# q's projection of six head pairs in the 512-column form, and the scaling of all probabilities on one engine

## The chip, the cores and the metric

The kernel runs on one core of a Trainium2 chip. The core has a matrix engine (TensorE, PE in the rows; its weight loads are listed apart as PEld), three engines for elementwise work (VectorE or DVE, ScalarE or ACT, GpSimd or POOL), and DMA queues that one more engine (SyncE, SP) starts. Each engine works through its own list of instructions in order and waits on semaphores for the others. The metric is the device time of one execution in microseconds, as the median of several runs.

## The reference

One layer of a decoder: RMS norm, 16-head causal attention over 256 positions with model width 1024, a residual, RMS norm, a gated feed-forward block of width 2816 with a causal three-tap convolution, a residual, and a last norm. With a sequence of 256 and blocks of 256 there is one block only, so the block choice of the attention drops out and what is left of it is

```
hn  = rmsnorm(x, norm_mix)
q   = hn @ Wq * 64**-0.5 ;  k = hn @ Wk ;  v = hn @ Wv      # 16 heads of 64
p   = softmax(causal(q @ k.T))                              # per head, 256 x 256
x   = x + (p @ v) @ w_o
x   = x + conv_ffn(rmsnorm(x, norm_ffn))
out = rmsnorm(x, norm_final)
```

All inputs and outputs are float32.

## The kernel before

Every large product is made from two parts of each operand: a high part (a copy rounded to the format that TensorE takes, written by ACT) and a low part (the operand minus its high part, written by DVE). Three matmuls then add up high x high, high x low and low x high in PSUM (`mm3`, lines 231 to 235). The transposed input lies in one tile `XT`, for each of its 8 slices of 128 rows the high part (256 columns) and right beside it the low part (256 columns).

There are two ways to project a weight slice. The narrow one (`proj`, line 244) issues three matmuls of 256 columns per slice. The wide one, used by the feed-forward block for its columns 3 to 20 (lines 579 to 581), issues one matmul of 512 columns, high weights times high and low input side by side, and one of 256 columns, low weights times high input. It leaves the sum in two halves of a PSUM bank, which are added on DVE afterwards (lines 635 and 636).

The attention works on pairs of heads, 0 to 7. The projections of pairs 0 and 1 are done while the first data arrive. Pairs 2 to 7 are done in ticks (`qk_tick`, line 483); between the ticks of pairs 5 and 6 stands one value tick, which projects the second half of v. A tick projects q (`A`) and k (`B`) of its pair, and in between does the scores and softmax of the pair two back and the transposes and p x v of the pair three back. What follows the tick of pair 7 is written out in a closing list, `LAST`.

The order is a list, `SCHED`, of named steps with a lag: lag 1 means that the step belongs to the tick before. Each step goes to the end of the lists of the engines that it uses, so the list fixes the order on every engine:

```
("OL", 1), ("KH", 1), ("QL", 1), ("H0", 0), ("KL", 1), ("L0", 0), ("A", 0), ("TR", 0), ("H1", 0),
("SC", 0), ("TH", 0), ("MX", 0), ("E0", 0), ("E1", 0), ("TL", 0), ("RC", 0), ("QH", 0), ("L1", 0),
("N0", 0), ("B", 0), ("KF", 0), ("N1", 0), ("H2", 0), ("PV", 0), ("OH", 0), ("L2", 0)
```

On ACT run `H` (high part of weights, line 180), `KH` and `QH` (high parts of k and q, lines 288 and 276), `E0`, `E1` (the exponentials, 321), `TH` (high part of the transposed probabilities, 346) and `OH` (high part of p x v, 362). On DVE run `L` (low part of weights, 183), `KF`, `KL`, `QL` (scaling of k, low parts of k and q; 284, 292, 280), `MX` (mask and maximum, 311), `RC` (reciprocal of the sums, 325), `TL` (349) and `OL` (367). The probabilities of query rows 0 to 127 and 128 to 255 are scaled by the reciprocals in `N0` (ACT, 128 columns, line 331) and `N1` (DVE, 256 columns, line 333), two instructions each. On TensorE the scores of a pair (`SC`) take as weights first the high part of k, and with their second matmul its low part, which `KL` writes; p x v takes with its second matmul the low part of the transposed probabilities, which `TL` writes.

Of the kernel before, what the change touches and what calls it, by code (L numbers as in the profile page):

```python
# [10 lines left out]
AF = mybir.ActivationFunctionType  # L11
ALU = mybir.AluOpType
AX = mybir.AxisListType

P = 128
S = 256
D = 1024
KT = D // P
# [32 lines left out]
def hybrid_layer(ctx: ExitStack, tc: tile.TileContext, a):  # L51
    nc = tc.nc
    pe, dve, act, pool = nc.tensor, nc.vector, nc.scalar, nc.gpsimd
# [7 lines left out]
    def f32(t):  # L61
        return t.bitcast(F32)

    def psA():
        return ps.tile([P, 512], F32, name="psA", tag="A", bufs=4)

    def psS(i):
        return ps.tile([P, 512], F32, name=f"psS{i}", tag=f"S{i}")
# [36 lines left out]
    XT = cst.tile([P, KT, 2, S], F32R, name="XT")  # L105
    XTh, XTl = XT[:, :, 0, :], XT[:, :, 1, :]
# [103 lines left out]
    QK = [Unit(a["wqk"][j - 2] if j > 1 else None, 2048, 2) for j in range(NP)]  # L210
    VW = [Unit(a["wv"][i], 2048, 2) for i in range(4)]
    WO = [Unit(a["wo"][j], 1024, 1) for j in range(NP)]
    UP = [Unit(a["wup"][c], 2048, 2) for c in range(NC)]
# [17 lines left out]
    def mm3(out, l, r, first, last):  # L231
        (lh, ll), (rh, rl) = l, r
        pe.matmul(out, lh, rh, start=first, stop=False)  # L233
        pe.matmul(out, lh, rl, start=False, stop=False)  # L234
        pe.matmul(out, ll, rh, start=False, stop=last)  # L235
# [8 lines left out]
    def proj(out, unit, k, off):  # L244
        h, l = unit.v(unit.hi, KT), unit.v(unit.lo, KT)
        mm3(out[:, :S], (h[:, k, off:off + P], l[:, k, off:off + P]), (XTh[:, k, :], XTl[:, k, :]),
            k == 0, k == KT - 1)
# [9 lines left out]
    def bcast_R(c, alloc):  # L257

        rp = alloc()
        for t in range(2):  # L260
            pe.transpose(rp[:, t * P:(t + 1) * P], st[:, c + t:c + t + 1].to_broadcast([P, P]), ident)
        act.activation(R, rp[:, :S], AF.Copy)
# [6 lines left out]
    qps, kps, SP, PR, PT, OP = {}, {}, {}, {}, {}, {}  # L269
    KF, QH, QL = {}, {}, {}  # L270
# [7 lines left out]
    def q_lo(j):  # L278
        QL[j] = wk.tile([P, S], F32R, name="QL", tag="ml", bufs=3)
        dve.tensor_sub(QL[j], qps[j][:, :S], f32(QH[j]))  # L280

    def k_evac(j):
        KF[j] = wk.tile([P, S], F32, name="KF", tag="QT")
        dve.tensor_mul(KF[j], kps[j][:, :S], R)

    def k_hi(j):
        for h in range(2):
            act.activation(KMh[j % 2][rows[h], h, :], KF[j][rows[h], :], AF.Copy)

    def k_lo(j):  # L290
        for h in range(2):
            dve.tensor_sub(KMl[j % 2][rows[h], h, :], KF[j][rows[h], :], f32(KMh[j % 2][rows[h], h, :]))
# [34 lines left out]
    def softmax_norm(j, t):  # L327
        for h in range(2):
            r = sm[j][:, 4 + 2 * t + h:5 + 2 * t + h]
            if t == 0:  # L330
                act.activation(PR[j][:, h, 0:P], PR[j][:, h, 0:P], AF.Copy, scale=r)
            else:
                dve.tensor_scalar(PR[j][:, h, P:P + S], PR[j][:, h, P:P + S], r, None, op0=ALU.mult)

    def transp(j):
        PT[j] = psT()
# [32 lines left out]
    def v_mm(half, part, vp, ts=(0, 1), kks=range(4)):  # L369
        u = VW[2 * half + part]  # L370
        h, l = u.v(u.hi, 4), u.v(u.lo, 4)
        for t in ts:
            for kk in kks:
                k = 4 * part + kk
                tk = slice(t * P, (t + 1) * P)
                mm3(vp[t], (XTh[:, k, tk], XTl[:, k, tk]), (h[:, kk, :], l[:, kk, :]), k == 0, k == KT - 1)
# [5 lines left out]
    def v_lo(half, vp, t):  # L382
        c = slice(half * 512, (half + 1) * 512)
        dve.scalar_tensor_tensor(Vl[:, t, c], vp[t], st[:, 2 + t:3 + t], f32(Vh[:, t, c]),
                                 op0=ALU.mult, op1=ALU.subtract)

    def qproj(j):
        qps[j] = psA()
        for k in range(KT):
            proj(qps[j], QK[j], k, 0)  # L390

    def kproj(j):
        kps[j] = psA()
# [7 lines left out]
    for k in range(KT):  # L401
        c = slice(S * k, S * k + S)
# [25 lines left out]
    def halves(u, key):  # L428
        return {f"{n}{key}{i}": (lambda f=f, i=i: f(i)) for n, f in (("H", u.split_hi), ("L", u.split_lo)) for i in range(u.n)}

    def scales():
# [3 lines left out]
    start = {"V0": lambda: v_mm(0, 0, vp), "V1": lambda: v_mm(0, 1, vp, (0,), (0, 1)), "V2": lambda: v_mm(0, 1, vp, (0,), (2, 3)),  # L435
             "V3": lambda: v_mm(0, 1, vp, (1,)), "KH0": lambda: k_hi(0), "KL0": lambda: k_lo(0),
             "RS": scales, "BC": lambda: bcast_R(2, lambda: psS(0)), **halves(VW[1], "V"), **halves(QK[2], "Q")}
    for i in range(2):
        start |= {f"QH{i}": lambda i=i: q_hi(i), f"QL{i}": lambda i=i: q_lo(i), f"KF{i}": lambda i=i: k_evac(i),
                  f"SS{i}": lambda i=i: ssq(x_sb[:, i, :], i, x1[:, i, :]),  # L440
                  f"VH{i}": lambda i=i: v_hi(0, vp, i), f"VL{i}": lambda i=i: v_lo(0, vp, i)}
# [19 lines left out]
    def steps(a_mm, b_mm, j, s_j, t_j, nxt):  # L461
        nxt = [(u, i) for u in nxt for i in range(u.n)]
        d = {"A": a_mm, "B": b_mm, "SC": lambda: scores(s_j), "MX": lambda: softmax_dve(s_j),
             "E0": lambda: softmax_exp(s_j, 0), "E1": lambda: softmax_exp(s_j, 1),
             "RC": lambda: softmax_recip(s_j), "N0": lambda: softmax_norm(s_j, 0), "N1": lambda: softmax_norm(s_j, 1),
             "KH": lambda: k_hi(s_j + 1), "KL": lambda: k_lo(s_j + 1)}
        for n, (u, i) in enumerate(nxt):
            d[f"H{n}"], d[f"L{n}"] = (lambda u=u, i=i: u.split_hi(i)), (lambda u=u, i=i: u.split_lo(i))
        if j is not None:
            d |= {"QH": lambda: q_hi(j), "QL": lambda: q_lo(j), "KF": lambda: k_evac(j)}  # L470
        if t_j is not None:
            d |= {"TR": lambda: transp(t_j), "TH": lambda: pt_hi(t_j), "TL": lambda: pt_lo(t_j), "PV": lambda: pv(t_j),
                  "OH": lambda: o_hi(t_j), "OL": lambda: o_lo(t_j)}
        return d
# [8 lines left out]
    def qk_tick(j, *args):  # L483
        tick(lambda: qproj(j), lambda: kproj(j), j, *args)
# [51 lines left out]
    for i in range(5):  # L536
        last[f"W{i}"] = lambda i=i: wo_all(i)
    last |= {"SC": lambda: scores(7), "MX": lambda: softmax_dve(7), "E0": lambda: softmax_exp(7, 0),
             "E1": lambda: softmax_exp(7, 1), "RC": lambda: softmax_recip(7), "N0": lambda: softmax_norm(7, 0),
             "N1": lambda: softmax_norm(7, 1), "Hc0": up2, "Lc0": lambda: UP[2].split_lo(0)}  # L540
    for i in (6, 7):
        last |= {f"TR{i}": lambda i=i: transp(i), f"TH{i}": lambda i=i: pt_hi(i), f"TL{i}": lambda i=i: pt_lo(i),
# [5 lines left out]
    gps = {}  # L548
# [19 lines left out]
    def wide(c):  # L568
        return 3 <= c < NC - 1


    def up(c, g, ks):
        if (c, g) not in gps:
            gps[c, g] = psA()
        for k in ks:
            if not wide(c):
                proj(gps[c, g], UP[c], k, g * P)
                continue
            h, l = (UP[c].v(t, KT)[:, k, g * P:(g + 1) * P] for t in (UP[c].hi, UP[c].lo))
            pe.matmul(gps[c, g], h, XT[:, k], start=k == 0, stop=False)  # L580
            pe.matmul(gps[c, g][:, :S], l, XTh[:, k, :], start=False, stop=k == KT - 1)  # L581

    for t in range(2):
        wo_mm(5, t, 0)
# [17 lines left out]
    UP[2].split_lo(1)  # L602
    xtr(1, 0)
    up(0, 0, range(4))
    xtr(1, 1)
    up(0, 1, range(4))
    up(1, 0, range(4))
    xsplit(1, (0, 1))
    xsplit(1, (2, 3))
# [235 lines left out]
```

## Time and profile before

| what | us |
|---|---|
| three runs | 314.21, 313.17, 313.20 |
| their median | 313.20 |
| the profiled execution, its own time | 313.81 |
| its span, first to last instruction | 312.1 |
| from the transposes of pair 6's tick to those of pair 7's | 8.49 |

The profile lists, for one execution, the busy time of each engine, the groups of instructions by line with their mean time and the idle time before them, and the chain of work that ended last. In the timeline each row is a start, a duration, the engine and line, output and input tiles, and in brackets how long the engine had sat idle and who released it. A matmul's duration overlaps with the next one; the spacing of starts is what it takes of TensorE. The granted TensorE clock was 0.997 of full speed over the span.

### The profile page before, as it was taken

To read this page: it belongs to the slowest core of one execution; us is meant where nothing else is said; L and a number is where in the kernel's file an instruction comes from. 1 tells how busy PE (TensorE), PEld (TensorE's weight loads), DVE (VectorE), ACT (ScalarE), POOL (GpSimd) and SP (SyncE) were. 2 spreads that over 40 slices of the span, in tenths; PEclk is the share of its full clock that TensorE was granted. 3 is DMA by queue.
4 is the path that set the end of the run, shared out by engine and by line. 5 is a ranking of instruction groups with operands and counts; after the bars stand their busy time and mean duration, and the time that the engine had idled before them with its cause. 6 is when DMAs were issued, how large, how long until landed. Compare 5 with 4: busy or idle time off the path is not lost.

```text
span 312.1 us, 4927 instructions
## 1 busy us (share of the span) xinstructions
PE 303.9 (97%) x1789; PEld 267.1 (86%) x1789; DVE 260.6 (84%) x515; ACT 213.4 (68%) x406; POOL 8.1 (3%) x26
## 2 busy tenths in 40 slices
PE   8899999999999999999999999999999999999991
PEld 5888999988998889998888888888888888888981
DVE  3776888977999977389998999998888888886885
ACT  5786878877989827477767777676666666664423
POOL 5000000000000000000000000000000000000021
PEclk9999999999999999999999999999999999999998
DMA  6999453873041594428764666555555511220003
GB/s 202 369 412 376 159 172 105 318 260 137 1 143 61 186 413 169 177 72 345 246 213 169 212 218 210 204 203 190 165 191 197 204 67 68 69 67 0 3 0 134
DMA packets 13944, 55.47 MB, mean 178 GB/s; under 512 B 1376, under 2 KB 4704, under 8 KB 10208
## 3 DMA queue, kind: packets, MB, share of 16 engines
q1 hardware_dynamic: 13344, 54.30, 48.0%
q10 hardware_dynamic: 576, 0.85, 0.8%
q8 instruction: 14, 0.23, 0.3%
q14 instruction: 10, 0.08, 0.1%
HBM read 54.10 MB, written 1.05 MB: 177 GB/s over the span
## 4 chain that ended last, share of the span: by engine, by line
PE 94%; DMA 2%; DVE 1%; SPq 1%; ACT 0%; issue 0%; DVEq 0%
PE psA L580 21%; PE psA L581 11%; PE psA L235 11%; PE psA L233 11%; PE psA L234 11%; PE psT L235 4%; PE psT L234 4%; PE psT L233 4%; PE psS L234 4%; PE psS L235 4%; PE psS L233 4%; DMA head<-in_first 2%; PE psT L339 2%; PE psA L415 1%; PE psA L419 1%; PE psA L417 1%
## 5 line engine op out<-in xcount | busy, mean ns | idle before, releaser
L580 PE MATMUL psA<-XT,whi 128*128 128x512 f32 x144 | 50.8, 393 | 0.0
L233 PE MATMUL psA<-XT,whi 128*128 128x256 f32 x144 | 40.8, 283 | 0.0
L235 PE MATMUL psA<-XT,wlo 128*128 128x256 f32 x144 | 40.6, 282 | 0.0
L234 PE MATMUL psA<-XT,whi 128*128 128x256 f32 x144 | 40.6, 282 | 0.0
L581 PE MATMUL psA<-XT,wlo 128*128 128x256 f32 x144 | 40.6, 282 | 0.0
L183 DVE TENSOR_TENSOR wlo<-head,whi 128x1024 fp32r<-128x1024 f32 x32 | 38.7, 1218 | 2.1 <-ACT whi L180 2.1
L648 DVE SCALAR_TENSOR_TENSOR y<-pad,head,y 128x256 f32<-128x256 f32 x86 | 36.1, 479 | 1.3 <-ACT y L643 1.3
L183 DVE TENSOR_TENSOR dlo<-rawd,dhi 128x1024 fp32r<-128x1024 f32 x29 | 35.3, 1218 | 0.1
L643 ACT ACTIVATE y<-pad,head 128x256 f32<-128x256 f32 x43 | 25.4, 598 | 13.6 <-DVE pad L637 10.2
L180 ACT ACTIVATE whi<-head 128x1024 fp32r<-128x1024 f32 x32 | 33.1, 1048 | 0.1
L580 PEld LDWEIGHTS psA<-XT,whi 128*128 128x128 f32 x144 | 27.0, 188 | 6.2
L180 ACT ACTIVATE dhi<-rawd 128x1024 fp32r<-128x1024 f32 x29 | 30.2, 1048 | 2.6 <-PE psA L235 2.1
L580 PE MATMUL psA<-XT,OTh 128*128 128x512 f32 x80 | 28.2, 393 | 0.0
L233 PEld LDWEIGHTS psA<-XT,whi 128*128 128x128 f32 x144 | 27.1, 189 | 0.4
L234 PEld LDWEIGHTS psA<-XT,whi 128*128 128x128 f32 x144 | 27.1, 188 | 0.4
L581 PEld LDWEIGHTS psA<-XT,wlo 128*128 128x128 f32 x144 | 27.1, 188 | 0.4
L235 PEld LDWEIGHTS psA<-XT,wlo 128*128 128x128 f32 x144 | 27.1, 188 | 0.0
L636 DVE TENSOR_TENSOR pad<-psA,pad 128x256 f32<-128x256 f32 x36 | 15.2, 423 | 13.8 <-ACT pad L635 13.8
L580 PE MATMUL psA<-XT,Vh 128*128 128x512 f32 x64 | 22.6, 393 | 0.0
L581 PE MATMUL psA<-XT,OTl 128*128 128x256 f32 x80 | 22.5, 282 | 0.0
L635 ACT ACTIVATE pad<-psA 128x256 f32<-128x256 f32 x36 | 12.7, 372 | 13.5 <-PE psA L581 13.5
L714 ACT ACTIVATE sact<-y 128x256 f32<-128x256 f32 x21 | 8.8, 419 | 16.9 <-DVE y L648 16.9
(201 smaller groups left out, 754.1 us busy)
## 6 DMA issues: line engine op xcount, KB each, us to landing
head<-in_wup SPq DMA_DIRECT2D x12, 1024.0 KB, 4.8
rawd<-in_wdn SPq DMA_DIRECT2D x22, 512.0 KB, 3.4
raw<-in_wup SPq DMA_DIRECT2D x10, 1024.0 KB, 4.8
raw<-in_wqk SPq DMA_DIRECT2D x4, 1024.0 KB, 7.5
rawd<-in_wo SPq DMA_DIRECT2D x8, 512.0 KB, 3.6
raw<-in_wv SPq DMA_DIRECT2D x4, 512.0 KB, 8.8
head<-in_wv SPq DMA_DIRECT2D x2, 1024.0 KB, 5.0
head<-in_first SPq DMA_DIRECT2D x5, 384.0 KB, 7.5
```

Of the source, the lines that this page charges most:

```text
L180: act.activation(self.hi[:, c], self.raw[:, c], AF.Copy)
L183: dve.tensor_sub(self.lo[:, c], self.raw[:, c], f32(self.hi[:, c]))
L233: pe.matmul(out, lh, rh, start=first, stop=False)
L234: pe.matmul(out, lh, rl, start=False, stop=False)
L235: pe.matmul(out, ll, rh, start=False, stop=last)
L580: pe.matmul(gps[c, g], h, XT[:, k], start=k == 0, stop=False)
L581: pe.matmul(gps[c, g][:, :S], l, XTh[:, k, :], start=False, stop=k == KT - 1)
L635: act.activation(u, v[:, S:], AF.Copy)
L636: dve.tensor_add(u, v[:, :S], u)
L643: act.activation(y[c, g], pads[c % 2][g][:, 2:S + 2], AF.Identity, scale=cw[:, 2, g * NC + c:g * NC + c + 1], bias=cb[:, g * NC + c:g * NC ...
L648: dve.scalar_tensor_tensor(y[c, g], pads[c % 2][g][:, j:j + S], cw[:, j, col:col + 1], y[c, g], op0=ALU.mult, op1=ALU.add)
L714: act.activation(sact, y[c, 0], AF.Silu)
```

## The change

For pairs 2 to 7 q's projection is issued in the wide form (a new `proj_wide`, now used by the feed-forward block too). q's high part is taken from the first half of the PSUM bank as before; to q's low part the second half is added by one more DVE instruction. `N1` goes from DVE to ACT, at the same place of `SCHED` and `LAST`; so all scaling of probabilities is on ACT. k's projection, pairs 0 and 1, and everything behind the attention compute as before. Lines after line 280 shift by a few.

```diff
     def q_lo(j):
         QL[j] = wk.tile([P, S], F32R, name="QL", tag="ml", bufs=3)
         dve.tensor_sub(QL[j], qps[j][:, :S], f32(QH[j]))
+        if j > 1:
+            dve.tensor_add(QL[j], qps[j][:, S:], f32(QL[j]))
...
     def softmax_norm(j, t):
         for h in range(2):
             r = sm[j][:, 4 + 2 * t + h:5 + 2 * t + h]
-            if t == 0:
-                act.activation(PR[j][:, h, 0:P], PR[j][:, h, 0:P], AF.Copy, scale=r)
-            else:
-                dve.tensor_scalar(PR[j][:, h, P:P + S], PR[j][:, h, P:P + S], r, None, op0=ALU.mult)
+            c = slice(0, P) if t == 0 else slice(P, P + S)
+            act.activation(PR[j][:, h, c], PR[j][:, h, c], AF.Copy, scale=r)
...
+    def proj_wide(out, unit, k, off):
+        h, l = (unit.v(t, KT)[:, k, off:off + P] for t in (unit.hi, unit.lo))
+        pe.matmul(out, h, XT[:, k], start=k == 0, stop=False)
+        pe.matmul(out[:, :S], l, XTh[:, k, :], start=False, stop=k == KT - 1)
+
     def qproj(j):
         qps[j] = psA()
         for k in range(KT):
-            proj(qps[j], QK[j], k, 0)
+            proj_wide(qps[j], QK[j], k, 0)
```

On ACT, in the tick of pair 6, before (`QH` is q's high part of pair 6, `dhi` the high part of a weight of the output projection, `OTh` that of p x v, `KMh_88` that of k):

```order
L276 ACTIVATE QH<-psA 128x256
L331 ACTIVATE PR<-PR,sm 128x128 x2
L180 ACTIVATE dhi<-rawd 128x1024
L362 ACTIVATE OTh<-psA 64x256 x2
L288 ACTIVATE KMh_88<-KF 64x256 x2
L180 ACTIVATE dhi<-rawd 128x1024 x2
L346 ACTIVATE pth<-psT 128x768
```

and now:

```order
L276 ACTIVATE QH<-psA 128x256
L333 ACTIVATE PR<-PR,sm 128x128 x2
L333 ACTIVATE PR<-PR,sm 128x256 x2
L180 ACTIVATE dhi<-rawd 128x1024
L362 ACTIVATE OTh<-psA 64x256 x2
L290 ACTIVATE KMh_88<-KF 64x256 x2
L180 ACTIVATE dhi<-rawd 128x1024 x2
```

The two scalings of 256 columns stand ahead of the weight's high part, and all that follows is behind them.

On DVE, same tick, before (`dlo` is the low part of that weight, `KMl_90` the low part of k that the next scores take):

```order
L325 RECIPROCAL sm<-sm 128x4
L183 TENSOR_TENSOR wlo<-raw_128,whi 128x1024
L284 TENSOR_TENSOR KF<-psA,R 128x256
L333 TENSOR_SCALAR PR<-PR,sm 128x256 x2
L183 TENSOR_TENSOR dlo<-rawd,dhi 128x1024
L367 TENSOR_TENSOR OTl<-psA,OTh 64x256 x2
L280 TENSOR_TENSOR QL<-psA,QH 128x256
L292 TENSOR_TENSOR KMl_90<-KF,KMh_88 64x256 x2
```

and now:

```order
L327 RECIPROCAL sm<-sm 128x4
L183 TENSOR_TENSOR wlo<-raw_128,whi 128x1024
L286 TENSOR_TENSOR KF<-psA,R 128x256
L183 TENSOR_TENSOR dlo<-rawd,dhi 128x1024
L367 TENSOR_TENSOR OTl<-psA,OTh 64x256 x2
L280 TENSOR_TENSOR QL<-psA,QH 128x256
L282 TENSOR_TENSOR QL<-psA,QL 128x256
L294 TENSOR_TENSOR KMl_90<-KF,KMh_88 64x256 x2
```

The scalings are gone, and the addition to q's low part stands between that low part and the low part of k.

On ACT, in the closing list, after the last exponentials (pair 7), before (`pth` is the high part of pair 6's transposed probabilities):

```order
L321 ACTIVATE PR,sm<-PR,mx 128x128 x2
L321 ACTIVATE PR,sm<-PR,mx 128x256 x2
L346 ACTIVATE pth<-psT 128x768
L180 ACTIVATE whi<-head 128x1024
L331 ACTIVATE PR<-PR,sm 128x128 x2
```

and now:

```order
L323 ACTIVATE PR,sm<-PR,mx 128x128 x2
L323 ACTIVATE PR,sm<-PR,mx 128x256 x2
L333 ACTIVATE PR<-PR,sm 128x256 x2
L346 ACTIVATE pth<-psT 128x768
L180 ACTIVATE whi<-head 128x1024
```

The scaling of pair 7 stands ahead of the high part of pair 6, and it has to wait for the reciprocals from DVE.

## Rows read from the trace of the kernel before

**Rows 1.** The page: busy time per engine; shares of the last-ending chain.
```profile
PE 303.9 (97%) x1789; PEld 267.1 (86%) x1789; DVE 260.6 (84%) x515; ACT 213.4 (68%) x406; POOL 8.1 (3%) x26
...
PE 94%; DMA 2%; DVE 1%; SPq 1%; ACT 0%; issue 0%; DVEq 0%
```
**Rows 2.** Windows: stretch; length; busy (count) of PE, PEld, DVE, ACT, POOL; clock; DMA.
```profile
78.65:87.14 8.49, 8.49 (x69) 8.22 (x68) 8.31 (x20) 8.11 (x21) 0.00 (x0) 1.00 0.07 12
```
**Rows 3.** PE timeline: 24 narrow matmuls from the first row, 15 wide steps from the third.
```profile
40.83 0.28 PE L233 MATMUL psA<-XT,whi 128*128 128x256 f32 x1
...
43.69 0.39 PE L233 MATMUL psA<-pth,Vh 128*128 128x512 f32 x1
...
149.67 0.39 PE L580 MATMUL psA<-XT,whi 128*128 128x512 f32 x1
...
154.92 0.40 PE L233 MATMUL psT<-dhi,mh 128*128 128x512 f32 x1
```
**Rows 4.** Groups by line and shape: busy us, mean ns, idle before.
```profile
L321 ACT ACTIVATE PR<-PR,mx 128x256 f32<-128x256 f32 x16 | 7.9, 497 | 0.0
...
L321 ACT ACTIVATE PR<-PR,mx 128x128 f32<-128x128 f32 x16 | 6.3, 394 | 1.2 <-DVE mx L311 1.2
...
L331 ACT ACTIVATE PR<-PR,sm 128x128 f32<-128x128 f32 x16 | 5.6, 394 | 0.2 <-DVE sm L325 0.2
...
L333 DVE TENSOR_SCALAR PR<-PR,sm 128x256 f32<-128x256 f32 x16 | 4.9, 348 | 0.0
```
**Rows 5.** DVE timeline, feed-forward: an addition and a product that reads its result.
```profile
166.80 0.42 DVE L636 TENSOR_TENSOR pad<-psA,pad 128x256 f32<-128x256 f32 x1 [1.27 <-ACT pad L635]
167.26 0.43 DVE L637 TENSOR_TENSOR pad<-pad,R 128x256 f32<-128x256 f32 x1
```
**Rows 6.** Timeline, pair 3's tick into pair 4's: ACT, DVE, scores' second matmul.
```profile
44.93 0.77 ACT L362 ACTIVATE OTh<-psA 64x256 fp32r<-64x256 f32 x2 [1.31 <-PE psA L235]
...
46.60 0.42 DVE L280 TENSOR_TENSOR QL<-psA,QH 128x256 fp32r<-128x256 f32 x1
46.94 0.86 DVE L292 TENSOR_TENSOR KMl<-KF,KMh 64x256 fp32r<-64x256 f32 x2
...
48.35 0.28 PE L234 MATMUL psS<-KMl,QH 128*128 128x256 f32 x1
```
**Rows 7.** Timeline, value tick: PEld (scores' second weights), then ACT.
```profile
68.13 0.19 PEld L234 LDWEIGHTS psS<-KMl,QH 128*128 128x128 f32 x1 [0.17 <-DVE KMl L292]
...
74.95 0.69 ACT L380 ACTIVATE Vh<-psA,st 128x512 fp32r<-128x512 f32 x1 [1.42 <-PE psA L235]
76.00 0.77 ACT L362 ACTIVATE OTh<-psA 64x256 fp32r<-64x256 f32 x2 [0.36 <-PE psA L235]
```
**Rows 8.** Timeline, pair 6's tick into pair 7's: ACT, DVE, scores' second matmul.
```profile
82.54 0.70 ACT L331 ACTIVATE PR<-PR,sm 128x128 f32<-128x128 f32 x2
83.14 1.05 ACT L180 ACTIVATE dhi<-rawd 128x1024 fp32r<-128x1024 f32 x1
84.45 0.77 ACT L362 ACTIVATE OTh<-psA 64x256 fp32r<-64x256 f32 x2 [0.27 <-PE psA L235]
...
84.39 1.22 DVE L183 TENSOR_TENSOR dlo<-rawd,dhi 128x1024 fp32r<-128x1024 f32 x1
...
86.73 0.86 DVE L292 TENSOR_TENSOR KMl<-KF,KMh 64x256 fp32r<-64x256 f32 x2
...
87.91 0.28 PE L234 MATMUL psS<-KMl,QH 128*128 128x256 f32 x1
```
**Rows 9.** Timeline, closing list: ACT, DVE, and the second matmul of p x v.
```profile
100.30 0.81 ACT L346 ACTIVATE pth<-psT 128x768 fp32r<-128x768 f32 x1
...
100.60 0.17 DVE L325 RECIPROCAL sm<-sm 128x4 f32<-128x4 f32 x1
...
101.34 0.95 DVE L349 TENSOR_TENSOR ptl<-psT,pth 128x768 fp32r<-128x768 f32 x1
...
102.96 0.39 PE L234 MATMUL psS<-ptl,Vh 128*128 128x512 f32 x1
```

More of the change, by code (lines that the diff above doesn't have):

```diff
@@ L575, in up @@
         for k in ks:
[L576 to L581, printed above, removed]
+            (proj_wide if wide(c) else proj)(gps[c, g], UP[c], k, g * P)
     for t in range(2):
```

## The prediction

> **What bounds the kernel now.** I read the page's engine table and its chain first. The chain is TensorE for 94% of the span and TensorE is busy for 97% [rows 1]; in the timeline its matmuls follow each other at a fixed spacing from the end of the start-up to the tail, through the attention too. So the end moves by what TensorE is spared, and by every moment that it is made to wait; a wait is never won back later, since no idle time follows in which to win it. Busy shares alone don't say how near such a wait is: over the stretch from pair 6's transposes to pair 7's, of 8.49 us, DVE is busy for 8.31 and ACT for 8.11 [rows 2]. There the question is which operand TensorE takes last, and how long before. For that I read the rows of the three engines around each place where TensorE takes something that the two others have just made: the low part of k (second matmul of the scores) and the low part of the transposed probabilities (second matmul of p x v).
>
> **The change part by part.**
>
> TensorE. A narrow step is three matmuls of 256 columns: 24 of them take 43.69 - 40.83 = 2.86 us, 0.3575 a step. A wide step of 512 and 256 columns takes (154.92 - 149.67) / 15 = 0.350 [rows 3]. The columns streamed are the same 768; one weight load and one start are saved, 0.0075 us. With 6 pairs of 8 slices: 48 x 0.0075 = 0.36 us gained, 0.06 a tick.
>
> The weight loads were hidden, then, in these rows. The Trainium skill ("TensorE: Matmul & The Clock Gate", LDWEIGHTS (loading the stationary operand)) prices a load of 128 columns at columns over 1.2 GHz, 107 ns, and its section Back-to-back issue gap lets load and matmul set the spacing together. If loads set it, 48 fewer would be 5.1 us by its figure, an estimate; the wide rows of this trace do not bear that out.
>
> q's low part. One DVE instruction per pair is added, reading PSUM and the result of the instruction before it. A pair of instructions so tied starts 167.26 - 166.80 = 0.46 apart [rows 5]; an untied follower starts 46.94 - 46.60 = 0.34 after [rows 6]. q's low part so takes 0.34 before and 0.46 + 0.34 = 0.80 now: +0.46 for all that stands behind it on DVE, first of all the low part of k.
>
> N1. DVE loses 16 instructions of 348 ns [rows 4]. Nobody on TensorE's path gets anything early for it, since where DVE stands before the places below, it waits for ACT. ACT gains 16 instructions that the trace does not show in this shape. The 128-column pair takes 83.14 - 82.54 = 0.60 from start to start [rows 8]; 128 columns more cost 497 - 394 = 103 ns each in the exponential [rows 4], so 0.60 + 0.21 = 0.81 a pair. Bounds: 0.60, as the pair of half the size, and 2 x 0.497 = 0.99, no overlap at all. I take 0.81.
>
> The Trainium skill ("ScalarE: Activation LUTs", Rules for kernel authors) speaks against this move: products belong on VectorE, not ScalarE. DVE's 348 ns against ACT's 394 for half the columns [rows 4] agree on the price. As a sum of engine time it would be about 8 x 0.3 = 2.4 us lost; which of it reaches the end is a matter of the places below.
>
> Now place by place, each behind the one before.
>
> Ticks up to pair 5. ACT waits for p x v anyway before its high part (1.31 us at 44.93 [rows 6]), and N1's 0.81 fits in. What remains is the 0.46. The low part of k ends at 46.94 + 0.86 = 47.80, and TensorE takes it at 48.35 [rows 6]; the hand-over costs 0.06, as in the value tick, where the weights start at 68.13 and the low part of k had ended 0.06 before. Slack 0.49, less 0.46, less the 0.06 by which the wide projection brings the scores nearer: -0.03. Each of the two ticks after pairs 3 and 4 loses 0.03. When the value tick comes, four wide projections have put TensorE 0.24 - 0.06 = 0.18 ahead.
>
> Value tick, scores. Here TensorE already waited 0.17 for the low part of k [rows 7]. The 0.46 goes straight on top, less the 0.18: TensorE is then 0.28 us later than before.
>
> Value tick, ACT. The second high part of v waits for TensorE (74.95) and ends at 75.64; then ACT was idle for 0.36, until p x v [rows 7]. N1 comes in between. From start to start it takes 0.81 and begins 0.09 before the end of its predecessor, as such pairs do (0.60 for two of 0.394 means 0.19 of overlap, half of it each): p x v's high part starts 0.36 later with respect to TensorE, 0.64 in all. Nothing on TensorE needs that yet; but the queue behind it, k's high part, two weight halves, the transposed probabilities and the exponentials of pair 6's tick, is back to back and carries the 0.64 along.
>
> Pair 6's tick. After its first scalings ACT has N1 once more: the weight's high part starts 0.64 + 0.81 = 1.45 late, at 84.59 instead of 83.14, and ends at 85.64. DVE, which began the low part of that weight at 84.39 [rows 8] with the high part long there, can now begin at 85.68, and it works in order: from there to the low part of k took 86.73 - 84.39 = 2.34, now 2.80. So the low part of k starts at 88.48, ends at 89.34, and TensorE has it at 89.40. It took it at 87.91 [rows 8]. TensorE is 1.49 us later than before, 1.27 of it a new wait (it would have come at 87.91 + 0.28 - 0.06). What DVE saved in N1 is spent waiting for that weight.
>
> Pair 7's tick. ACT again waits for TensorE ahead of p x v, as in the earlier ticks, and N1 fits there. All keeps step with TensorE.
>
> Closing list. N1 of pair 7 now precedes the high part of pair 6's transposed probabilities, and it needs the reciprocals. These end at 100.60 + 0.17 = 100.77 on DVE, so N1 runs from 100.80 and the high part starts at 101.61 instead of 100.30 [rows 9], ending at 102.42. DVE makes the low part from 102.44 on, 0.95 long, and with the hand-over it is there at 103.45; TensorE took it at 102.96 [rows 9]. Another 0.49. The next transposes and p x v of pair 7 come just in time by the same reckoning; behind them ACT idles again for TensorE.
>
> Sum: 1.49 + 0.49 = 1.98 us, the 0.36 of the wide form included. With N1 at 0.60 the places give 0.15, 1.07 and 0.28, in all 1.35; at 0.99 they give 0.54, 1.85 and 0.67, in all 2.52. The profiled execution took 313.81 (span 312.1), 0.6 above the median of the runs. I put the sum on the median: 313.2 + 2.0 = 315.2 us, from 314.5 to 315.8 by these bounds.
>
> **The rivals.**
>
> Hidden. Late operands are still in time, because ACT and DVE catch up in the idle stretches ahead of p x v (1.31, 0.36 and 0.27 us in the rows), and DVE has two instructions of 348 ns less to do in each tick. For it: the mean loads of ACT, 68% of the span. Against it: pair 6's tick leaves ACT 0.38 us and N1 wants 0.81, and the low part of k there had only 87.91 - 87.59 = 0.32 to spare, of which the addition alone takes 0.46. It decides if ACT reaches pair 6's weight less than about 0.2 late. Then only the wide form counts, with perhaps the 0.46 of the value tick: 313.2 - 0.36 = 312.8, or 313.3.
>
> Half. One of the two large waits does not appear, the closing list's or half of pair 6's: 313.2 + 0.5 to 1.4, about 314.2.
>
> Faster. Weight loads do set TensorE's spacing in this stage: 48 of them at the narrow spacing of 0.119 would be 5.7 us, 307.5. Against it stand the wide rows; a stage in which TensorE waits for nothing else would have to behave unlike the feed-forward block.
>
> Worse. The 0.49 us of slack in the ticks of pairs 4 and 5 is not there, as when the tied addition takes longer on a PSUM half that was just written: two waits of about 0.4 more, 316.0.
>
> **How the numbers follow.** The runs before differ by 1 us, so 0.5% (1.57 us) is about what can be told from no change: slower means over 314.8, faster under 311.6. Forecast 0.58, of it 0.52 over the bound; worse 0.08, all over; half 0.14, of it 0.02 over; hidden 0.16; faster 0.04. That makes slower 0.62, same 0.34, faster 0.04. The range of 8 in 10 leaves out the faster case and a tail above: 312.7 to 316.6; the forecast's own is 314.5 to 315.8.
>
> **What would show it.** In the profile after: q's projection at 0.350 a step; N1 on ACT at about 0.5 us, 0.4 apart; TensorE's weight loads waiting for the low part of k in the value tick (0.5 to 0.6 us) and in pair 7's tick (over 1 us); a wait for the low part of the transposed probabilities after the closing list's first transposes (about 0.5); from there to the end the timeline of before, shifted by 2 us. The forecast is wrong if pair 7's scores start without a wait, or if the stretch behind the attention is shorter or longer than before.

## The result and the profile after

The changed kernel takes 315.88 us (median of four runs, 315.86 to 316.92), the kernel before 313.39 in the same session (four runs, 313.17 to 314.21). The ratio is 1.0079, interval 1.0065 to 1.0094: 2.5 us slower. The time is 0.7 above the forecast of 315.2, inside the range of 8 in 10 (312.7 to 316.6) and 0.1 above the forecast's own bounds (314.5 to 315.8); the difference is 2.49 where the sum had 1.98.

The page of the changed kernel answers to [rows 1]: 48 matmuls and weight loads are gone, DVE has 16 instructions less and 6 more, ACT 16 more. The share of TensorE in the chain falls from 94 to 78%, those of ACT, DMA and DVE rise to 6, 6 and 5%. That tells along which work the chain is followed back, not how much was lost; the places below tell that.

```profile
PE 304.7 (97%) x1741; PEld 264.6 (84%) x1741; DVE 258.8 (82%) x505; ACT 219.5 (70%) x422; POOL 8.1 (3%) x26
...
PE 78%; ACT 6%; DMA 6%; DVE 5%; issue 1%; SPq 1%; POOL 0%; DVEq 0%; POOLq 0%
```

Columns of the windows as in [rows 2]; first the same stretch as there (now 8.39), then the two behind it. Before, TensorE was busy through all three, of 8.49, 9.46 and 7.17. Now the second has 1.12 in which it does nothing, the third 0.45. The second and the third before:

```profile
87.14:96.60 9.46, 9.46 (x62) 8.39 (x61) 8.91 (x22) 8.19 (x21) 0.00 (x0) 1.00 0.45 159
96.60:103.77 7.17, 7.17 (x37) 6.07 (x36) 7.10 (x17) 7.14 (x17) 0.00 (x0) 1.00 0.00 0
```

All three now:

```profile
79.47:87.86 8.39, 8.39 (x61) 7.80 (x60) 7.06 (x17) 8.28 (x22) 0.00 (x0) 1.00 0.01 3
87.86:98.69 10.83, 9.71 (x62) 8.45 (x61) 10.29 (x25) 9.85 (x23) 0.00 (x0) 1.00 0.44 146
98.69:106.61 7.92, 7.47 (x38) 6.00 (x36) 6.07 (x14) 7.37 (x18) 0.00 (x0) 1.00 0.01 2
```

The groups by shape (answering to [rows 4]) and the TensorE timeline of the wide q of one tick (to [rows 3]): N1 costs 496 ns on ACT, the added DVE instruction 424 ns, and eight wide steps take 47.76 - 44.97 = 2.79, or 0.349 a step.

```profile
L333 ACT ACTIVATE PR<-PR,sm 128x256 f32<-128x256 f32 x16 | 7.2, 496 | 0.5 <-DVE sm L327 0.5
...
L282 DVE TENSOR_TENSOR QL<-psA,QL 128x256 fp32r<-128x256 f32 x6 | 2.5, 424 | 0.2
```

```profile
44.97 0.39 PE L390 MATMUL psA<-XT,whi 128*128 128x512 f32 x1
...
47.76 0.82 PE L339 MATMUL psT<-ident,PR 128*128 128x128 f32 x6
48.33 0.36 PE L233 MATMUL psS<-KMh,QH 128*128 128x256 f32 x1
48.55 0.39 PE L234 MATMUL psS<-KMl,QH 128*128 128x256 f32 x1
48.77 0.28 PE L235 MATMUL psS<-KMh,QL 128*128 128x256 f32 x1
```

The last three rows are the scores in pair 4's tick [rows 6]. The low part of k comes so narrowly that TensorE shows no idle time. But the next matmul starts 0.22 behind the second one, where it was 0.12 before (48.47 after 48.35 in the same tick). The next row is that matmul before; the two behind it are the weight loads of the second and third matmul now:

```profile
48.47 0.28 PE L235 MATMUL psS<-KMh,QL 128*128 128x256 f32 x1
...
48.55 0.19 PEld L234 LDWEIGHTS psS<-KMl,QH 128*128 128x128 f32 x1
48.66 0.19 PEld L235 LDWEIGHTS psS<-KMh,QL 128*128 128x128 f32 x1
```

The late load starts together with its matmul (48.55), the load behind it 0.11 later, and that one's matmul another 0.11 later: the weights that would have been loaded ahead were not. I call these 0.10 the refill.

The value tick and pair 7's tick, answering to [rows 7] and [rows 8]. PEld, ACT and DVE in the first; TensorE, ACT and DVE in the second:

```profile
68.99 0.19 PEld L234 LDWEIGHTS psS<-KMl,QH 128*128 128x128 f32 x1 [0.63 <-DVE KMl L294]
...
76.39 0.90 ACT L333 ACTIVATE PR<-PR,sm 128x256 f32<-128x256 f32 x2
77.19 0.75 ACT L362 ACTIVATE OTh<-psA 64x256 fp32r<-64x256 f32 x2
...
83.71 1.50 ACT L333 ACTIVATE PR<-PR,sm 128x128 f32<-128x128 f32 x4
85.12 1.04 ACT L180 ACTIVATE dhi<-rawd 128x1024 fp32r<-128x1024 f32 x1
...
86.19 1.23 DVE L183 TENSOR_TENSOR dlo<-rawd,dhi 128x1024 fp32r<-128x1024 f32 x1 [1.07 <-ACT dhi L180]
...
88.20 0.42 DVE L280 TENSOR_TENSOR QL<-psA,QH 128x256 fp32r<-128x256 f32 x1
88.65 0.42 DVE L282 TENSOR_TENSOR QL<-psA,QL 128x256 fp32r<-128x256 f32 x1
89.00 0.86 DVE L294 TENSOR_TENSOR KMl<-KF,KMh 64x256 fp32r<-64x256 f32 x2
...
89.91 0.39 PE L234 MATMUL psS<-KMl,QH 128*128 128x256 f32 x1 [1.12 <-DVE KMl L294]
90.13 0.28 PE L235 MATMUL psS<-KMh,QL 128*128 128x256 f32 x1
```

The wait of 0.17 for KMl in the value tick is now 0.63. In pair 6's tick N0 and N1 together (the row with x4, which gives the shape of its first instruction) take 1.41 from start to start (85.12 - 83.71), the weight's high part is late, DVE stands idle for 1.07, and TensorE waits 1.12 for KMl.

The closing list, answering to [rows 9]:

```profile
102.69 0.17 DVE L327 RECIPROCAL sm<-sm 128x4 f32<-128x4 f32 x1
...
102.89 0.91 ACT L333 ACTIVATE PR<-PR,sm 128x256 f32<-128x256 f32 x2 [0.52 <-DVE sm L327]
103.83 0.81 ACT L346 ACTIVATE pth<-psT 128x768 fp32r<-128x768 f32 x1
...
104.67 0.96 DVE L349 TENSOR_TENSOR ptl<-psT,pth 128x768 fp32r<-128x768 f32 x1 [1.81 <-ACT pth L346]
...
105.68 0.50 PE L234 MATMUL psS<-ptl,Vh 128*128 128x512 f32 x1 [0.45 <-DVE ptl L349]
106.02 0.39 PE L235 MATMUL psS<-pth,Vl 128*128 128x512 f32 x1
```

To place the loss I take the starts of the transposes of pairs 0 to 7 (TR0 to TR7) and of the row transposes that end the stage behind the attention: 39.12, 67.22, 78.65, 87.14, 96.60, 103.77 and 128.03 before (TR0, TR3 to TR7, end of the stretch), 39.37, 67.62, 79.47, 87.86, 98.69, 106.61 and 131.02 after. What follows the last one takes 184.0 in both profiles. What precedes TR0 differs between executions: it comes at 38.3 to 39.4 in the twelve profiles of this study, so I leave the start-up out. Behind the value tick the lag is shorter than in the ticks before it: the ticks of pairs 6 and 7 do the scores and softmax of pairs 5 and 6 and the transposes of pairs 4 and 5. So N1 of pair 4 lies in the value tick, that of pair 5 in pair 6's tick, that of pair 6 in pair 7's, that of pair 7 in the closing list.

| stretch | before | after | difference | forecast |
|---|---|---|---|---|
| TR0 to TR3 (ticks of pairs 4 and 5) | 28.10 | 28.25 | +0.15 | -0.06 |
| TR3 to TR4 (value tick's scores) | 11.43 | 11.85 | +0.42 | +0.40 |
| TR4 to TR5 | 8.49 | 8.39 | -0.10 | -0.06 |
| TR5 to TR6 (pair 7's tick's scores) | 9.46 | 10.83 | +1.37 | +1.27 |
| TR6 to TR7 (closing list) | 7.17 | 7.92 | +0.75 | +0.49 |
| TR7 to the end of the stage | 24.26 | 24.41 | +0.15 | 0 |
| sum | 88.91 | 91.65 | +2.74 | +2.04 |

The last column puts the prediction's terms on these stretches. Its sum was 1.98: 0.12 of the wide gain lies ahead of TR0, and between the value tick's scores and pair 7's it took off one wide projection of 0.06 where two lie.

### The profile page after: what moved, and what is told of

Read it like the earlier page. It is cut to its first block, busy times and chain, and to the rows that moved or that the text cites. A ratio compares the mean times of both kernels' runs of the same rounds, so it can differ in the third digit from the quotient of the medians.

```text
span 315.1 us, 4839 instructions
## 1 busy us (share of the span) xinstructions
PE 304.7 (97%) x1741; PEld 264.6 (84%) x1741; DVE 258.8 (82%) x505; ACT 219.5 (70%) x422; POOL 8.1 (3%) x26
## 4 chain that ended last, share of the span: by engine, by line
PE 78%; ACT 6%; DMA 6%; DVE 5%; issue 1%; SPq 1%; POOL 0%; DVEq 0%; POOLq 0%
PE psA L390 23%; PE psA L391 12%; PE psA L235 6%; PE psA L234 6%; PE psA L233 6%; PE psS L234 4%; PE psS L235 4%; PE psS L233 4%; PE psT L235 4%; PE psT L234 4%; PE psT L233 4%; DMA x_sb<-in_x 3%; DMA head<-in_first 2%; DVE wlo L183 2%; ACT PR L333 1%
## 5 line engine op out<-in xcount | busy, mean ns | idle before, releaser
L390 PE MATMUL psA<-XT,whi 128*128 128x512 f32 x192 | 67.9, 393 | 0.0
L390 PEld LDWEIGHTS psA<-XT,whi 128*128 128x128 f32 x192 | 36.1, 188 | 8.0
L233 PE MATMUL psA<-XT,whi 128*128 128x256 f32 x96 | 27.3, 284 | 0.0
L234 PE MATMUL psA<-XT,whi 128*128 128x256 f32 x96 | 27.1, 282 | 0.0
L233 PEld LDWEIGHTS psA<-XT,whi 128*128 128x128 f32 x96 | 18.1, 189 | 0.3
L234 PEld LDWEIGHTS psA<-XT,whi 128*128 128x128 f32 x96 | 18.1, 188 | 0.3
```

Of the source, the lines that this page charges most:

```text
L390: pe.matmul(out, h, XT[:, k], start=k == 0, stop=False)
```

## The experiments

Ten kernels ran, each timed in five rounds beside the kernel before (whose median was 313.55, 313.42 and 313.49 in the three sessions). The last column is the difference of the stretch from TR0 to the end of the stage against 88.91, from the profile of each; TR4 to TR5 and what follows TR7 have no column of their own. In these kernels some lines lie three or so further down.

| kernel | median us | ratio to before | TR0-TR3 | TR3-TR4 | TR5-TR6 | TR6-TR7 | whole stretch |
|---|---|---|---|---|---|---|---|
| changed kernel | 315.88 | 1.0079 (1.0065-1.0094) | +0.15 | +0.42 | +1.37 | +0.75 | +2.74 |
| e1 wide and addition only | 314.73 | 1.0048 (1.0028-1.0068) | +0.12 | +0.38 | +0.74 | +0.03 | +1.29 |
| e2 N1 on ACT only | 315.39 | 1.0059 (1.0044-1.0074) | +0.01 | 0.00 | +0.82 | +0.74 | +1.70 |
| e3 pair 7's N1 on DVE | 315.71 | 1.0066 (1.0051-1.0081) | +0.17 | +0.39 | +1.37 | +0.01 | +1.89 |
| e4 as e1, QL behind KL | 313.76 | 1.0013 (1.0001-1.0025) | -0.13 | -0.31 | +0.74 | +0.01 | +0.23 |
| e5 N1 of pairs 4, 5 on DVE | 315.54 | 1.0063 (1.0050-1.0075) | +0.10 | +0.43 | +0.43 | +0.75 | +1.79 |
| e6 before, QL behind KL | 313.38 | 0.9998 (0.9987-1.0009) | 0.00 | -0.25 | 0.00 | +0.03 | -0.23 |
| e8 e4, N1 mixed | 313.45 | 0.9998 (0.9988-1.0007) | -0.11 | -0.28 | +0.50 | +0.03 | +0.05 |
| e9 e8, L2 later | 314.20 | 1.0025 (1.0015-1.0036) | -0.13 | -0.31 | +1.12 | 0.00 | +0.68 |
| e10 e8, pair 6 narrow | 313.90 | 1.0008 (0.9992-1.0023) | -0.13 | -0.25 | 0.00 | +0.03 | -0.35 |
| e11 wide, no addition | 313.26 | 0.9991 (0.9977-1.0004) | -0.10 | -0.04 | +0.01 | +0.03 | -0.21 |

The changed kernel's time by the ratio, 2.48, is 0.26 below its stretch; it ran four times, in a session of its own. For the others, e10 aside, the time by the ratio lies between 0.11 below and 0.22 above the stretch. A step between two kernels is therefore read from the traces.

**The two halves of the change.** e1, N1 as before:

```
-            act.activation(PR[j][:, h, c], PR[j][:, h, c], AF.Copy, scale=r)
+            if t == 1:
+                dve.tensor_scalar(PR[j][:, h, c], PR[j][:, h, c], r, None, op0=ALU.mult)
+            else:
+                act.activation(PR[j][:, h, c], PR[j][:, h, c], AF.Copy, scale=r)
```

> The changed kernel with all N1 back on DVE: only q's wide projection and the addition to q's low part are left of the change. Theory (late operands at three places): the closing list's wait and ACT's delay in pair 6's tick go; what stays is the addition's 0.46 us ahead of the low part of k, which shows as a wait in the value tick (about 0.4 to 0.5 us with the 0.17 of before) and a small one in pair 7's tick (0.2 to 0.3); with the 0.36 gained by the wide form 313.7 to 314.1 us. Rival (the addition and the wide form carry the loss, N1 is hidden): about 315.4 to 315.9.

e2, q as before, N1 on ACT:

```
-                dve.tensor_scalar(PR[j][:, h, P:P + S], PR[j][:, h, P:P + S], r, None, op0=ALU.mult)
+                act.activation(PR[j][:, h, P:P + S], PR[j][:, h, P:P + S], AF.Copy, scale=r)
```

> The kernel before with all N1 on ACT and nothing else changed (narrow projection, no addition). Theory: ACT's delay alone makes the scores of pair 7's tick wait 0.7 to 0.8 us and the closing list's p x v 0.5 to 0.6, the value tick waits as before (0.17); 314.6 to 315.0 us. So the two halves alone add up to less than the change (0.5 + 1.4 against 2.5), since both lie on the same chain in pair 6's tick and slack pays for part of each only once. Rival (N1 is hidden): 313.4. Rival (N1 alone carries all): 315.9.

Both came out slower than expected, by 0.6 and 0.4 past the expected range. The places are the expected ones: e2 loses nothing up to TR5, then 0.82 in pair 7's tick and 0.74 in the closing list; e1 loses in the value tick. But e1 also loses 0.74 in pair 7's tick, where I had expected 0.2 to 0.3. W0, which `LAST` puts into that stretch, is the output projection's part for pair 0: four groups of matmuls (`dhi`, `dlo` times `OTh`, `OTl`), each with an accumulator of its own. PEld and DVE of e1 there:

```profile
88.56 0.19 PEld L234 LDWEIGHTS psS<-KMl,QH 128*128 128x128 f32 x1 [0.34 <-DVE KMl L294]
...
95.02 0.19 PEld L233 LDWEIGHTS psA<-dhi,OTh 128*128 128x128 f32 x1 [0.40 <-issue]
95.78 0.19 PEld L233 LDWEIGHTS psA<-dhi,OTh 128*128 128x128 f32 x1 [0.24 <-issue]
...
94.48 0.42 DVE L282 TENSOR_TENSOR QL<-psA,QL 128x256 fp32r<-128x256 f32 x1
94.82 0.85 DVE L370 TENSOR_TENSOR OTl<-psA,OTh 64x256 fp32r<-64x256 f32 x2
```

The windows of e1 say why (columns as above): DVE is busy for 10.00 of 10.20 us.

```profile
87.48:97.68 10.20, 10.06 (x62) 8.38 (x61) 10.00 (x25) 8.58 (x21) 0.00 (x0) 1.00 0.43 149
```

With N1 and the addition both on DVE, DVE is the bound of that stretch: KMl is late, and later the weight loads of W0's third and fourth group start 0.12 and 0.11 after QL and the second OL end on DVE (94.48 + 0.42 = 94.90, and 94.82 + 0.85 = 95.67). The profile names no releaser there; that it is the accumulators which QL and OL had to free is what e8 tests. So what N1's move gives DVE is not worthless, though the prediction counted it so. The two halves add up to more than the change (1.29 + 1.70 = 2.99 against 2.74), not to less, as the expectation of e2 had it.

**Pair 7's N1**, e3 (in the changed kernel):

```
-            act.activation(PR[j][:, h, c], PR[j][:, h, c], AF.Copy, scale=r)
+            if t == 1 and j == 7:
+                dve.tensor_scalar(PR[j][:, h, c], PR[j][:, h, c], r, None, op0=ALU.mult)
+            else:
+                act.activation(PR[j][:, h, c], PR[j][:, h, c], AF.Copy, scale=r)
```

> The changed kernel with N1 of pair 7 alone back on DVE (the one in the closing list); the other seven stay on ACT. Theory: the closing list's wait for the low part of the transposed probabilities goes, 0.6 to 0.7 us as the trace of the changed kernel has it, all else stays: 315.2 us. Rival (ACT's load as a whole, each N1 a like share): one eighth of N1's part, 0.2 to 0.3, so 315.6. Rival (the scores' waits alone set the end, and the closing list has slack behind it): 315.9.

In the trace it does what was expected: the closing list's 0.75 goes to 0.01 and 0.14 behind it with it, all other stretches stay. The ratio improves by less (0.0013 of 313.4, 0.4 us) than the 0.85 of the trace; both intervals leave room for either. The median, 315.71, lies nearer to the rivals' 315.6 and 315.9 than to the 315.2 of the theory, so the timing does not decide between them. The trace does: a like share for each N1, or slack behind the closing list, would not take away that list's loss alone and whole.

**The order of QL and KL**, e4, from e1, and its control e6, from the kernel before:

```
-    ("OL", 1), ("KH", 1), ("QL", 1), ("H0", 0), ("KL", 1), ("L0", 0), ...
+    ("OL", 1), ("KH", 1), ("H0", 0), ("KL", 1), ("QL", 1), ("L0", 0), ...
```

> q's projection wide, all N1 on DVE, and in SCHED the step QL (q's low part, with its addition) moved from ahead of KL to behind it, so that the low part of k no longer stands behind q's. Theory: no wait is left at the scores, the 0.17 of before goes as well, the wide form's 0.36 is gained: 312.7 to 312.9 us, faster than both kernels. Rival (the wide form itself costs, in TensorE's time or by PSUM banks that are held longer): 313.5 to 314.5, with waits at k's projection or at the first matmul of a bank.

> The kernel before with one edit: QL stands behind KL in the ticks' list (narrow q, no addition, N1 on DVE as before). A control for the reordered run with the wide form. Theory: the kernel before has one wait for KMl, in the value tick (0.17 at 68.13, 0.32 with the refill behind it); with KL first it goes, nothing else changes: 313.2 against 313.5 for the kernel before (-0.2 to -0.4). So the reordered wide kernel (313.76) is slower than the same order with narrow q, since DVE is full in pair 7's tick. Rival: QL comes too late for the third matmul of the scores: 313.6 to 314.0.

With KL first every wait for KMl is gone (TR0 to TR3 -0.13 instead of +0.12, TR3 to TR4 -0.31 instead of +0.38). This shows that the addition's cost up to the value tick comes from standing ahead of KL. But e4 was to be faster than both kernels and is not: its 313.76 lies in the rival's range, and pair 7's tick still costs 0.74, 0.43 of it now as a wait for QL with its refill and most of the rest at W0's late groups. If those wait for accumulators, as e8 and e9 will show, the rival's banks that are held longer were in part right. e6 shows the order alone: the trace gains 0.25 in the value tick, the timing can't tell it from nothing.

**N1 of pairs 4 and 5**, e5, the changed kernel with `if t == 1 and j in (4, 5)` on DVE:

> The changed kernel with N1 of pairs 4 and 5 back on DVE; N1 of the other pairs on ACT, wide form and addition kept. Theory, as the first four runs leave it: in pair 7's tick the changed kernel's wait for KMl (1.12 us by its row) had two parts, ACT's later KMh (N1 of pair 5) and QL's addition; with N1 of pair 5 on DVE the addition's part stays, 0.3 to 0.5 with the refill as in the run with the wide form alone; the value tick's wait stays at 0.43 and the one in the closing list for ptl at 0.45. Against 313.5 for the kernel before: 315.2 (314.9 to 315.5). Rival A, the addition alone makes the wait in pair 7's tick: no change from the changed kernel, 315.9. Rival B, N1 of pair 4 also makes the value tick's wait: that falls by 0.3 or more as well, 314.7.

The trace has it as the theory had. Pair 7's tick falls from +1.37 to +0.43: N1 of pairs 4 and 5 on ACT makes the larger part of that wait, the addition the rest. The edit takes both pairs' N1 away at once. In the changed kernel the weight's high part starts 1.16 later behind TR4 (85.12 - 79.47 against 83.14 - 78.65), and 0.81 of that is pair 5's own N1, so at most 0.35 is left for pair 4's. The time, 315.54, is just above the expected range (314.9 to 315.5) and alone would not tell the theory from rival A. TensorE there and, for comparison, DVE and ACT of e2 with N1 alone:

```profile
88.62 0.39 PE L234 MATMUL psS<-KMl,QH 128*128 128x256 f32 x1 [0.16 <-DVE KMl L294]
88.84 0.29 PE L235 MATMUL psS<-KMh,QL 128*128 128x256 f32 x1
```

```profile
82.83 1.50 ACT L331 ACTIVATE PR<-PR,sm 128x128 f32<-128x128 f32 x4
84.24 1.04 ACT L180 ACTIVATE dhi<-rawd 128x1024 fp32r<-128x1024 f32 x1
...
85.31 1.22 DVE L183 TENSOR_TENSOR dlo<-rawd,dhi 128x1024 fp32r<-128x1024 f32 x1 [1.07 <-ACT dhi L180]
```

In e2 DVE waits the same 1.07 for the weight's high part, with no addition in the kernel. The value tick's loss stays (+0.43), so N1 of pair 4 has no part in that one.

**Each N1 where its engine has time**, e8, from e4: N1 of pairs 4, 5 and 7 on DVE, of the others on ACT.

```
-            if t == 1:
+            if t == 1 and j in (4, 5, 7):
```

> Wide q and addition, QL behind KL, N1 of pairs 4, 5 and 7 on DVE, of pairs 0 to 3 and 6 on ACT. Theory: in the reordered run with all N1 on DVE, DVE ran without a gap through pair 7's tick, and W0's third and fourth group waited 0.29 in sum for the accumulators that QL and OL free; N1 of pair 6 on ACT stands in ACT's idle time there (0.87 ahead of OH) and takes 0.52 off DVE, so the 0.29 goes: 313.45 (313.3 to 313.6), the same as the kernel before. QL's wait of 0.17 with its refill stays in that tick. Rival: those W0 groups wait for something else (WO's weights): 313.8, as the reordered run.

Met: 313.45. W0's third group starts on time again and the weight load of the fourth waits 0.19, about the 0.17 (at 94.72) of the kernel before; in e4 the two waits were 0.38 and 0.24. The load of the fourth group starts 0.11 or 0.12 after the second OL ends on DVE in the kernel before, e1, e4, e8 and e9 alike, whenever that is, and so does that of the third after QL where QL is late (e1, e4, e9). With that the accumulators' part is shown, and what is left is QL. PEld of e8:

```profile
87.10 0.19 PEld L235 LDWEIGHTS psS<-KMh,QL 128*128 128x128 f32 x1 [0.39 <-DVE QL L282]
...
93.94 0.19 PEld L233 LDWEIGHTS psA<-dhi,OTh 128*128 128x128 f32 x1 [0.19 <-issue]
```

**L2 out of the way**, e9, from e8 (L2 is in pair 6's tick the low part of the output projection's first weight, `WO[0]`):

```
-    ("OL", 1), ("KH", 1), ("H0", 0), ("KL", 1), ("QL", 1), ("L0", 0), ...
+    ("OL", 1), ("KH", 1), ("H0", 0), ("KL", 1), ("QL", 1), ("L2", 1), ("L0", 0), ...
...
-    ("N1", 0), ("H2", 0), ("PV", 0), ("OH", 0), ("L2", 0)
+    ("N1", 0), ("H2", 0), ("PV", 0), ("OH", 0)
```

> As the mixed run, and L2 of pair 6's tick (the low part of WO[0], 1.13 us of DVE) moved from ahead of OL, KL and QL to right behind them. Theory, DVE's order is what TensorE waits for in pair 7's tick: OTl, KMl and QL come 1.1 earlier, QL's wait and refill (0.35 in sum) go, and WO[0] is still ready 3 us before W0 reads it: 313.05 (312.8 to 313.3), faster than the kernel before by 0.4 and the mixed run by 0.35. Rival: WO[0]'s buffer is freed 2.6 us later, its successor's DMA lands later and a split in the closing list waits: 313.5 to 314.5.

Slower, though not by the rival's DMA: no wait of ACT or DVE over 0.1 us from TR5 to the end of the stage is for one. DVE of e9, and TensorE and PEld behind it:

```profile
84.13 0.86 DVE L370 TENSOR_TENSOR OTl<-psA,OTh 64x256 fp32r<-64x256 f32 x2 [0.74 <-ACT OTh L365]
...
86.72 2.35 DVE L183 TENSOR_TENSOR dlo<-rawd,dhi 128x1024 fp32r<-128x1024 f32 x2
```

```profile
91.35 0.50 PE L234 MATMUL psA<-ptl,Vh 128*128 128x512 f32 x1 [0.33 <-DVE ptl L352]
...
92.95 0.19 PEld L233 LDWEIGHTS psA<-dhi,OTh 128*128 128x128 f32 x1 [0.26 <-DVE KF L286]
```

QL is just in time now. But L2 had filled the time in which DVE waits for p x v: DVE idles there for 0.74, OL, KL and QL come only some 0.3 earlier instead of 1.1, and MX and TL, behind both L steps, come late. W0's second group waits too, and there the profile names the releaser: KF, which W0 does not read, so what is waited for is the accumulator that KF empties.

**Pair 6 narrow**, e10, from e8:

```
+WIDE_Q = (2, 3, 4, 5, 7)
-        if j > 1:
+        if j in WIDE_Q:
             dve.tensor_add(QL[j], qps[j][:, S:], f32(QL[j]))
-            proj_wide(qps[j], QK[j], k, 0)
+            (proj_wide if j in WIDE_Q else proj)(qps[j], QK[j], k, 0)
```

> The mixed run with q of pair 6 in the narrow form again and its QL without the addition; pairs 2 to 5 and 7 stay wide. Theory: in pair 7's tick it is QL of pair 6 that comes late (wait 0.19 for QL, 0.45 with its refill), because DVE has no gap there; without the addition of 0.46 that wait goes, the wide gain of 0.06 of that tick is lost, and the stretch from pair 6's TR to the next is 9.5 long in place of 9.96: 313.05 (312.8 to 313.3) against 313.4 for the kernel before, 0.4 faster than it and the mixed run. Rival: what is late there hangs on DVE's order and not on the addition (as when L2 was moved): 313.4, no change.

In the trace it is as expected: TensorE stands idle nowhere from TR0 to the end of the stage, pair 7's tick takes 9.46 as before, DVE is busy for 8.92 of it, and the stretch is 0.35 shorter than before, the shortest of all.

```profile
86.22:95.68 9.46, 9.46 (x62) 8.38 (x61) 8.92 (x22) 9.09 (x23) 0.00 (x0) 1.00 0.46 159
```

The time doesn't follow: 313.90 against 313.49, with runs from 312.84 to 315.22; -0.35 us would be a ratio of 0.9989, just outside the interval. The runs show two reasons. The medians of the spans, first to last instruction, are 311.75 and 311.8, the same; the time outside the span is 1.7 or 1.8 in every run of the kernel before, but 2.0 to 3.1 in seven of the twelve runs of e10, and why is open. And in the one execution with a profile most of the gain is lost again behind the stage, which takes 184.3 instead of 184.0:

```profile
299.19 0.19 PEld L768 LDWEIGHTS psT<-whi,mh 128*128 128x128 f32 x1 [0.41 <-issue]
```

e9 has the same 184.3, the other ten profiles 184.0 or 184.1; the wait there has no named releaser. From TR0 to the last instruction e10 takes 272.9, as the kernel before does. I can't claim a version that beats the kernel before.

**The wide form alone**, e11, from e1:

```
         dve.tensor_sub(QL[j], qps[j][:, :S], f32(QH[j]))
-        if j > 1:
-            dve.tensor_add(QL[j], qps[j][:, S:], f32(QL[j]))
```

> The wide form of q's projection alone: N1 on DVE and the order of the kernel before, and the addition left out (the correction stays in the upper half of the accumulator and is used by nothing). Theory: what is left of the change is 48 steps at 0.0075 us, 0.36 at most; some of it is lost at the value tick, where KMl and not TensorE sets the time: 313.15 (313.0 to 313.4) against 313.4 before; so that of the run with wide form and addition (+1.2 to 1.5) all comes from the addition. Rival: the wide form itself costs time (its last matmul ends later, QH and QL start later): 313.8 or more.

The kernel then uses q's low part without the correction in the bank's second half. As expected: 0.21 less in the trace, most of it outside the value tick, where KMl sets the time (PEld of e11, the same wait as in [rows 7]):

```profile
67.64 0.19 PEld L234 LDWEIGHTS psS<-KMl,QH 128*128 128x128 f32 x1 [0.16 <-DVE KMl L292]
```

The timing can't tell it from no change. Against e1 the addition alone is worth 1.50 us in the trace: 0.22 in the ticks, 0.42 in the value tick, 0.73 in pair 7's, the rest scatter.

## Why the prediction was right in kind and too small

- TensorE bounds the kernel and never wins a wait back: right. What follows the stage is as long before as after, 184.0.
- In the prediction's bounds (0.15, 1.07 and 0.28; 0.54, 1.85 and 0.67) the first figure is ACT's delay in the value tick and goes into the second; only the second and third are added.
- The wide form, 0.0075 us a step: right (0.349 a step; e11). The Trainium skill's price for weight loads ("TensorE: Matmul & The Clock Gate", LDWEIGHTS (loading the stationary operand)) would have made 48 fewer worth 5.1 us, an estimate; here the loads are hidden, and e11 gains 0.21 in the stretch from TR0, in which four of the six wide projections lie.
- The addition, 0.46 ahead of KL: right to 0.01 (88.65 - 88.20 and 89.00 - 88.65, in sum 0.80). The value tick's term came as forecast, +0.42 for +0.40.
- N1 at 0.81 a pair: right where ACT runs through (77.19 - 76.39 = 0.80; 1.41 for N0 and N1). In the closing list it takes 103.83 - 102.89 = 0.94. The two scalings last as long there (0.91, in the value tick 0.90), but the next instruction on ACT starts 0.03 after their end, in the value tick 0.10 before it; why is not shown.
- Pair 7's tick, the largest term: 1.27 forecast, 1.37 found; e5 and e2 show the mechanism, late weight in pair 6's tick and addition behind it.
- Mis-sized: "Each of the two ticks after pairs 3 and 4 loses 0.03." The waits there are that small, but each late weight load costs the refill of 0.10 as well. TR0 to TR3 so grew by 0.15 instead of shrinking by 0.06; e1 has +0.12 there, and e4, which differs from it only in that KMl comes early, has -0.13. That is 0.21 of the missing 0.70.
- Mis-sized: the closing list, "Another 0.49." Found 0.75 and another 0.15 behind it: N1's 0.13 more, the refill twice (105.68 to 106.02 is 0.34 instead of 0.23; behind pair 7's low part 110.27 to 110.58 is 0.31 instead of 0.22), and 0.08 that I can't place. That is 0.41. What is left of the 0.70, another 0.08, is pair 7's tick with its own refill (+0.10) and scatter.
- "Nobody on TensorE's path gets anything early for it" (DVE's relief from N1): wrong for pair 7's tick. DVE was at 8.91 of 9.46 there before; the addition without the relief costs 0.74 in that stretch (e1), with N1 of pair 6 taken off 0.43 to 0.50 (e5, e8). It changed no term of the sum, since the change did bring the relief, but it made me expect e1 and e4 too fast.
- The rule that products belong on VectorE (the Trainium skill, "ScalarE: Activation LUTs", Rules for kernel authors) agrees with the price of one instruction, 496 against 348 ns. It doesn't decide here: in the stretch of pair 6's N1, N1 on ACT saves 0.24 (e8 against e4, which differ in pairs 0 to 3 too), pair 7's costs 0.85 (e3 in the trace).

## What to carry to other kernels

Where one engine bounds and two others feed it closely, price an edit at each hand-over by which instruction it stands ahead of, not by engine time: q's low part with its addition costs 0.94 us less up to TR4 when it stands one step later (e4 against e1; 0.25 of that q's low part gains without the addition too, e6), and the same scaling gains for pair 6 and loses for pair 7. Add to each new wait on a weight load the refill behind it. Before counting an engine's relief as worthless, look whether another part of the change fills that engine.

## What the runs showed of the hardware

- A matmul whose weights come late is followed by a second gap: the next starts 0.22 instead of 0.12 behind it for 256 columns (0.34 instead of 0.23 for 512), also where the late one shows no idle time.
- Two scalings of 256 columns on ACT last 0.90 and 0.91, but the next instruction starts 0.80 after the first of them in the value tick and 0.94 after it in the closing list.
- A group of matmuls can wait for its accumulator, at its first weight load: 0.40 and 0.24 in e1, 0.12 and 0.11 after DVE last read the accumulators. The rows show no releaser for such a wait in e1, and KF in e9.
- The changed kernel and e3 have the same instructions up to TR0 and reach it at 39.37 and 38.52: a start-up differs by more between executions than most terms of this change. Such terms can be read from a stretch of one trace, hardly from medians.
